# Differential attention on one core: stores from ScalarE's queue, loads in blocks, high parts first, and the norm factor by Newton's iteration on GpSimd

## The chip, the core and the metric

The kernel runs on one core of a Trainium2 chip. The metric is device time in microseconds (us) of one launch. The engines are named as in the profile: PE is TensorE's matmul, PEld its weight load, DVE is VectorE, ACT is ScalarE, POOL is GpSimd, SP is SyncE, which here only issues DMAs (SPq in a trace row; a DMA that ScalarE issues stands as ACTq).

## The reference

One layer of an encoder over two sequences (512 tokens and a second of the same length in the kernel's layout), width 1024, fp32: an S5 scan branch, a differential-attention branch and a cross-attention branch, gated and merged, then a gated FFN. The change lies in the differential attention and in the merge of its neighbours:

```python
def _diff_attention(q, k, v, lam, subln_g, lambda_init):
    ...
        s = jnp.einsum('bqhd,bkhd->bhqk', qblk, k).astype(jnp.float32) * scale
        probs = jax.nn.softmax(s, axis=-1).reshape(Bn, DIFF_HEADS, 2, Q_BLOCK, L)
        w = probs[:, :, 0] - lam * probs[:, :, 1]
        return jnp.einsum('bhqk,bkhe->bqhe', w.astype(v.dtype), v)
    ...
    o = _rmsnorm(o, subln_g) * (1.0 - lambda_init)
    return o.reshape(Bn, L, DIFF_WIDTH)

def _layer(x, mem, l, p):
    ...
    branches = (y_s5, y_diff, y_x)
    merged = None
    for n in range(N_BRANCH):
        term = jax.nn.sigmoid(g[..., n * D_MODEL:(n + 1) * D_MODEL]) * (branches[n] @ p['w_up'][l, n])
        merged = term if merged is None else merged + term
    x = x + merged @ p['w_out'][l]
```

## The kernel before

**Precision.** A product of fp32 values is made from three matmuls on parts: a value is cast on ScalarE to a high part (names ending in h or H) and VectorE subtracts that from it for the low part (l or L). The products are high by high, low by high and high by low; `mm3` issues them for the projections.

**Stages.** The S5 branch and the cross attention come first. The differential attention fills about 505 to 770 us of the span. It has 4 heads, 2 sequences and 4 query tiles of 128 rows, so 32 `steps`. Between its pieces, TensorE is kept at work by other units of the layer: projections of the next heads' q and k, of v, of the gates, and the merge of branches 0 and 2 (`units`, `qk_units`, `gate_units`, `merge_units`). They stand in `queue`, and `fill(n)` pulls from it.

**A step.** `score(i)` issues the scores of both maps of a step (PE into `bksc`, three banks in turn), VectorE's maximum `nb`, ScalarE's two exps `e`, and on VectorE the difference of the two maps and a transposition in blocks; the result is stored to `eD` in DRAM. For every second step `turn(i)` reads the pair of steps back from `eD` with four DMAs (`tn`), which completes the transposition. Such two steps are called a pair here: pair p holds steps 2p and 2p + 1. `settle` later issues the split of `tn` into pH (ScalarE's cast) and pL (VectorE's subtraction), and `outputs(i)`, three loop turns after the pair's second step, multiplies them by v in 12 matmuls into `bkoo`. After a head's four query tiles, `squares` makes the sums of squares `ss` (by TensorE's transposition and ScalarE's squares), and `normed` the factor: ScalarE's square root, VectorE's reciprocal, four transposes on TensorE that spread it over the partitions (`bktr`), VectorE's product, and a store to `bD`, from which the merge of branch 1 reads after the stage.

**Keys and queries.** A projection of q or k is rotated on VectorE and GpSimd; its split and its DMAs (tile `hl` to `q`, or to `h` and `l`, eight DMAs for each half of a key tile) are held back in a closure, `finished`, which `rotate` runs.

**Order.** A scheduler of the tile framework chooses the order of instructions on ScalarE, VectorE, GpSimd and SyncE from the program and its own costs. TensorE keeps the program's order here (`PE.on`). `tc.issue_after(x)` makes the instructions within it stand behind x where both are of the same engine. SyncE and ScalarE issue their instructions and DMAs strictly in the order so chosen, so one that waits holds all behind it.

Of the kernel before, what the change touches and what calls it, by code (L numbers as in the profile page):

```python
# [9 lines left out]

F32 = mybir.dt.float32
F32R = mybir.dt.float32r
I32 = mybir.dt.int32
AF = mybir.ActivationFunctionType
ALU = mybir.AluOpType
# [4 lines left out]
P = 128  # L20
L = 512
DM = 1024
KD = DM // P
# [47 lines left out]
def encoder(ctx: ExitStack, tc: tile.TileContext, a, out, out_t):  # L71
# [49 lines left out]
    wf = wp.tile([P, DM], F32, tag="wf", name="wf")  # L121
# [75 lines left out]

    last_mm = None

    def mm3(outs, wh, wl, xs, k, nk):  # L200

        nonlocal last_mm
        ws = slice(k * P, (k + 1) * P)
# [43 lines left out]
    def factor(ss, n, nt=4, bias=epsc):  # L247
        rs = root(ss, n, nt, bias)
        return rs, spread(rs, nt)
# [117 lines left out]
    o = bank()  # L367
# [344 lines left out]
        while any(g is g_ for g_ in queue):  # L712
            fill(1)

    def units(src, use, nk=KD, hl=lambda: (xh, xl)):

        wf = weight_in(src, nk * P)
        yield 0
        hi, lo = hl()
        wh, wl = weight_split(wf, nk * P)  # L720
        for s in range(NS):
            cs = slice(s * L, (s + 1) * L)
            o = bank()
            for k in range(nk):
                mm3([o], wh, wl, [(hi[k][:, cs], lo[k][:, cs])], k, nk)
# [128 lines left out]
    def rotate(*behind):  # L854
        with ExitStack() as es_:
            for b in behind:
                es_.enter_context(tc.issue_after(b.ins))
            while turning:
                turning.pop(0)()

    def rotated(is_q, first=False):


        names = (("q0", "q1"), ("h0", "h1", "l0", "l1"))[not is_q]
        tiles = [slot("qk", [P, NT], F32R, n_) for n_ in names]
        top, bottom = slice(0, 64), slice(64, P)

        def use(s, o):
            cs = slice(s * L, (s + 1) * L)
            t1 = rp.tile([P, L], F32, tag="nsq", name="t1", bufs=2) if first else ap_.tile([P, L], F32, tag="t1", name="t1", bufs=1)  # L870
            V.tensor_tensor(out=t1, in0=o, in1=rope[0], op=ALU.mult)
            t2 = ap_.tile([P, L], F32, tag="t2", name="t2", bufs=1)
            V.stream_shuffle(t2, o, mask)
            PO.tensor_tensor(out=t2, in0=t2, in1=rope[1], op=ALU.mult)
            PO.tensor_tensor(out=t1, in0=t1, in1=t2, op=ALU.add)
            def finished():
                hl = slot("ld", [P, 2, L], F32R, "hl")
                if is_q:
                    split(hl[:, 0], hl[:, 1], t1, scale=0.125)
                else:  # L880
                    split(*(by_row(hl[:, j], 4) for j in range(2)), by_tile(t1, 4))
                for mp in range(2):
                    for j in range(2):
                        src = hl[MAPS[mp], j].bitcast(F32)
                        if is_q:
                            SP.dma_start(tiles[mp].bitcast(F32)[MAPS[j], cs], src)
                        else:
                            for rows in (top, bottom):
                                SP.dma_start(tiles[2 * j + mp].bitcast(F32)[rows, cs], src)
# [30 lines left out]
        return list(zip(*(merge_part(n, t, tags[t]) for t in range(4))))  # L920

    def merge_units(n, b, m, first=False, last=False):
        u = units(a["w_up"][n, m], lambda s, o: use(s, o), 4, b)
        yield next(u)
        gt = slot("ld", name="gl")
        SP.dma_start(gt, gD[n * KD + m])
# [62 lines left out]
    def score(i):  # L989
        nonlocal last_e  # L990
        h, s, qt = steps[i]
        cs = slice(s * L, (s + 1) * L)
        if h and s == qt == 0:
            finish(dk[h])
            rotate()
        if qt == 0:
            s0[h, s] = acol.tile([P, 4], F32, tag="s0", name="s0", bufs=3)
        q_, k_, er = qk[h, True], qk[h, False], []
        qs_ = slice(s * L + qt * P, s * L + (qt + 1) * P)
        sc = [bank("sc") for _ in MAPS]  # L1000
        for mp in range(2):
            PE.matmul(sc[mp], q_[mp][:, qs_], k_[mp][:, cs], start=True, stop=False)
            PE.matmul(sc[mp], q_[mp][:, qs_], k_[2 + mp][:, cs], start=False, stop=True)
        for mp in range(2):
            er.append(softmax_parts(ap_, acol, sc[mp], L, 1.0, f"d{mp}", None if mp else s0[h, s][:, qt : qt + 1]))
        (e0, sm0), (e1, r1) = er
        V.scalar_tensor_tensor(out=r1, in0=r1, scalar=nlam, in1=sm0, op0=ALU.mult, op1=ALU.mult)
        V.scalar_tensor_tensor(out=e0, in0=e1, scalar=r1, in1=e0, op0=ALU.mult, op1=ALU.add)
        last_e = last_x, V.transpose(e1, e0)
        SP.dma_start(eD[i // 2 % 4, i % 2], e1)  # L1010

    def turn(i):
        h, s, qt = steps[i]
# [4 lines left out]
    def outputs(i):  # L1018

        h, s, qt = steps[i]  # L1020
        if h == 2 and s == qt - 1 == 0:
            finish(v1_)
        vh, vl = (v1 if h >= 2 else v0)[s]
        vs = slice((h % 2) * P, (h % 2) * P + P)
        pH, pL = pT.pop((h, s, qt // 2))
        if qt == 1:
            osb[h, s] = bank("oo")
        od = osb[h, s][:, qt // 2 * 2 * P : (qt // 2 + 1) * 2 * P]
        for j in range(4):
            PE.matmul(od, vh[:, j, vs], pH[:, j, :], start=(j == 0), stop=False)  # L1030
            PE.matmul(od, vh[:, j, vs], pL[:, j, :], start=False, stop=False)
            PE.matmul(od, vl[:, j, vs], pH[:, j, :], start=False, stop=(j == 3))
        if qt == 3:
            o_ = rp.tile([P, L], F32, tag="nsq", name="osb", bufs=2)
            S.copy(o_, osb[h, s])
            osb[h, s] = o_

    def squares(i):
# [9 lines left out]
        V.scalar_tensor_tensor(out=s0[h, s], in0=s0[h, s], scalar=EPS * P, in1=s0[h, s], op0=ALU.mult, op1=ALU.mult)  # L1048
        V.tensor_tensor(out=ss[h, s], in0=ss[h, s], in1=s0[h, s], op=ALU.add)

    def normed(i):
        h, s, _ = steps[i]
        _, bc = factor(ss[h, s], P, bias=0.0)
        V.scalar_tensor_tensor(out=osb[h, s], in0=osb[h, s], scalar=g04, in1=bc, op0=ALU.mult, op1=ALU.mult)
        SP.dma_start(bD[1, h, :, s * L : (s + 1) * L], osb[h, s])

    n = len(steps)
    for i in range(-1, n + 6):
        if i + 1 < n:
            score(i + 1)  # L1060
            settle(last_x)
            rotate(last_x)
        if i in (22, 23):
            first_in(2 * i - 44)
        fill(10)
        if i in (21, 22):
            first_in(3 if i == 21 else 1)
        if 0 <= i < n:
            turn(i)
        if 3 <= i < n + 3 and steps[i - 3][2] % 2:  # L1070
            outputs(i - 3)
# [1129 lines left out]
```

## Time and profile before

| | |
|---|---|
| median of 3 runs (lowest, highest) | 1571.77 us (1570.17, 1572.47) |
| the profiled execution: its time, its span | 1569.32 us, 1567.5 us |
| granted TensorE clock | 0.999 |
| busy share of the span: PE, PEld, DVE, ACT, POOL | 99%, 83%, 73%, 41%, 33% |
| the stage at 505 to 770 us: PE, DVE, ACT, POOL busy | 260.36, 207.61, 134.66, 47.58 us of 265.00 |
| exps of the stage on ACT | 64 of 686 ns |
| table loads of the stage on ACT | 13 of 1283 ns |

A row of the timeline gives the start (us of the span), the duration (us), the engine, the line, the operation, its output and inputs by the program's names, the tile, and in brackets how long the engine had been idle before and what ended that. In rows by group, the number behind the bar is the sum of busy time, then the mean in ns of one, then the idle time ahead of the group and what ended it. In a tile's rows, three numbers with slashes are the shortest, median and longest in ns. A row of waits gives the sum, the count and the mean in us. L62 is the line of the helper through which every engine's instructions are issued, so it doesn't tell operations apart; their tiles do.

### The profile page before, as it was taken

To read this page: it belongs to the slowest core of one execution; us is meant where nothing else is said; L and a number is where in the kernel's file an instruction comes from. 1 tells how busy PE (TensorE), PEld (TensorE's weight loads), DVE (VectorE), ACT (ScalarE), POOL (GpSimd) and SP (SyncE) were. 2 spreads that over 40 slices of the span, in tenths; PEclk is the share of its full clock that TensorE was granted. 3 is DMA by queue.
4 is the path that set the end of the run, shared out by engine and by line. 5 is a ranking of instruction groups with operands and counts; after the bars stand their busy time and mean duration, and the time that the engine had idled before them with its cause. 6 is when DMAs were issued, how large, how long until landed. Compare 5 with 4: busy or idle time off the path is not lost.

```text
span 1567.5 us, 21345 instructions
## 1 busy us (share of the span) xinstructions
PE 1553.6 (99%) x7505; PEld 1302.6 (83%) x7505; DVE 1141.2 (73%) x1769; ACT 637.0 (41%) x1109; POOL 513.5 (33%) x406
## 2 busy tenths in 40 slices
PE   9999999999999999999999999999999999999998
PEld 8888888888898888887888888888888888788887
DVE  6797689665774888877556567777777777999664
ACT  7354323344773356564223353333333323333222
POOL 0001000001443220200443345667665542445352
PEclk9999999999999999999999999999999999999999
DMA  9543372566897666577544324555433342786632
GB/s 364 205 148 136 105 254 103 177 179 217 278 306 221 176 204 185 172 239 266 189 148 170 139 94 143 185 177 175 155 122 134 115 154 77 261 292 203 208 118 107
DMA packets 162491, 286.22 MB, mean 183 GB/s; under 512 B 34768, under 2 KB 91344, under 8 KB 162384
## 3 DMA queue, kind: packets, MB, share of 16 engines
q1 hardware_dynamic: 160944, 280.64, 53.9%
q10 hardware_dynamic: 1440, 4.22, 0.7%
q8 instruction: 59, 0.97, 0.2%
q14 instruction: 48, 0.39, 0.1%
HBM read 185.47 MB, written 86.74 MB: 174 GB/s over the span
## 4 chain that ended last, share of the span: by engine, by line
PE 83%; DVE 6%; DMA 6%; issue 2%; ACT 2%; SPq 1%; DVEq 0%; ACTq 0%
PE bkmm L62 74%; PE bktr L62 7%; SPq L62 1%; DMA yt<-bD 1%; PE bksc L62 1%; PE bkoo L62 1%; DVE e L62 1%; DMA tn<-eD 1%; DVE wl L62 1%; DVE nb L62 1%; DMA c_n<-cD 1%; ACT e L62 1%; DMA eD<-e 1%; DMA zu<-uD 1%; DVE t L62 1%
## 5 line engine op out<-in xcount | busy, mean ns | idle before, releaser
L62 PE MATMUL bkmm<-xl,wh 128*128 128x512 f32 x640 | 250.7, 392 | 0.0
L62 PE MATMUL bkmm<-xh,wh 128*128 128x512 f32 x640 | 250.5, 392 | 0.0
L62 PE MATMUL bkmm<-xh,wl 128*128 128x512 f32 x640 | 249.6, 390 | 0.3 <-DVE wl L62 0.2
L62 PE MATMUL bkmm<-th,whl 128*128 128x512 f32 x696 | 227.3, 390 | 0.0
L62 ACT CAST wh<-wf 128x1024 fp32r<-128x1024 f32 (+1 forms) x131 | 116.0, 886 | 194.6 <-PE bkmm L62 164.2
L62 DVE TENSOR_TENSOR wl<-wf,wh 128x1024 fp32r<-128x1024 f32 (+1 forms) x132 | 141.5, 1073 | 54.7 <-ACT wh L62 52.1
L62 PEld LDWEIGHTS bkmm<-th,whl 128*128 128x128 f32 x696 | 130.6, 188 | 27.3 <-issue 0.2
L62 PEld LDWEIGHTS bkmm<-xh,wl 128*128 128x128 f32 x640 | 120.2, 188 | 26.2 <-DVE wl L62 1.1
L62 PE MATMUL bkmm<-th,w 128*128 128x512 f32 x432 | 139.6, 390 | 1.1 <-DVE nsq L62 1.1
L62 PEld LDWEIGHTS bkmm<-xh,wh 128*128 128x128 f32 x640 | 120.3, 188 | 24.1 <-issue 0.2
L62 PEld LDWEIGHTS bkmm<-xl,wh 128*128 128x128 f32 x640 | 120.3, 188 | 23.8 <-issue 0.6
L62 POOL TENSOR_TENSOR raw<-raw 128x128 f32<-128x128 f32 x144 | 92.2, 641 | 143.5 <-DMA raw<-in_w_fo 96.4
L62 PE MATMUL bkmm<-tl,whl 128*128 128x512 f32 x348 | 135.4, 389 | 0.0
L62 POOL TENSOR_TENSOR ws<-wf 128x512 f32<-128x512 f32 x44 | 72.6, 1650 | 146.0 <-DMA wf<-in_w_fu 139.1
L62 DVE TENSOR_TENSOR whl<-ws,whl 128x1024 fp32r<-128x1024 f32 x44 | 74.5, 1693 | 60.8 <-ACT whl L62 60.8
L62 PE MATMUL bkmm<-th,wh 128*128 128x512 f32 x260 | 101.3, 390 | 0.0
L62 PE MATMUL bkmm<-th,wl 128*128 128x512 f32 x260 | 101.2, 389 | 0.0
L62 PE MATMUL bkmm<-tl,wh 128*128 128x512 f32 x260 | 101.2, 389 | 0.0
L62 PEld LDWEIGHTS bkmm<-th,w 128*128 128x128 f32 x432 | 81.0, 188 | 19.1 <-DVE nsq L62 1.5
L62 POOL TENSOR_TENSOR mg<-mg,gl 128x1024 f32<-128x1024 f32 x16 | 44.2, 2762 | 131.8 <-DVE gl L62 127.1
L62 ACT ACTIVATE e<-bksc,nb 128x512 f32<-128x512 f32 (+1 forms) x96 | 58.7, 614 | 69.4 <-DVE nb L62 64.3
L62 PE MATMUL bkmm<-tl,w 128*128 128x512 f32 x216 | 84.0, 389 | 0.0
(644 smaller groups left out, 3580.2 us busy)
## 6 DMA issues: line engine op xcount, KB each, us to landing
wf<-in_w_in SPq DMA_DIRECT2D x40, 512.0 KB, 4.7
wD<-hl SPq DMA_DIRECT2D x36, 512.0 KB, 3.0
w<-wD SPq DMA_DIRECT2D x36, 512.0 KB, 3.9
gD<-gt SPq DMA_DIRECT2D x24, 512.0 KB, 3.1
gl<-gD SPq DMA_DIRECT2D x24, 512.0 KB, 3.8
raw<-in_w_fo SPq DMA_DIRECT2D x88, 128.0 KB, 3.5
wf<-in_w_fg SPq DMA_DIRECT2D x22, 512.0 KB, 3.9
wf<-in_w_fu SPq DMA_DIRECT2D x22, 512.0 KB, 3.5
```

The lines of the kernel that those rows point to most:

```text
L62: ins = do(*args, **kw)
```

## The change

It has five parts.

- Stores: the DMA that stores a step's result to `eD` is issued by ScalarE instead of SyncE for 31 of the 32 steps, and one step later, behind the second exp of the next step. `score` returns it as a closure.
- SyncE's order: the h and l DMAs stand behind the last load of `tn` that was issued before them, `rotate` runs after `turn`, and weight loads and gate loads get a position behind TensorE's last matmul of `mm3`. As that instruction is TensorE's and these DMAs are SyncE's, this last position changes no engine's order.
- High parts first: `outputs` issues the eight matmuls with pH, then the four with pL.
- Merge of branch 0: the row blocks are taken in the order 3, 0, 1, 2, which is the order in which they are loaded.
- Norm factor: `newton` on GpSimd makes one over the square root in 14 operations on 128x4 (a first value from the bits of the number, and three iterations), in place of ScalarE's square root and VectorE's reciprocal; `normed` runs one loop turn later. With the square roots, 13 table loads of ScalarE between 572 and 729 us go; one is added ahead of the next square root after the stage, that of `rs<-bktr` at 924 us.

The number of matmuls is the same. SyncE has 31 instructions fewer, ScalarE 11 more (31 DMAs in, square roots and table loads out), GpSimd 112 more, VectorE 8 fewer.

```diff
-        SP.dma_start(eD[i // 2 % 4, i % 2], e1)
+        return lambda: (S if i % 32 < n - 1 else SP).dma_start(eD[i // 2 % 4, i % 2], e1)
...
         for j in range(4):
             PE.matmul(od, vh[:, j, vs], pH[:, j, :], start=(j == 0), stop=False)
-            PE.matmul(od, vh[:, j, vs], pL[:, j, :], start=False, stop=False)
-            PE.matmul(od, vl[:, j, vs], pH[:, j, :], start=False, stop=(j == 3))
+            PE.matmul(od, vl[:, j, vs], pH[:, j, :], start=False, stop=False)
+        for j in range(4):
+            PE.matmul(od, vh[:, j, vs], pL[:, j, :], start=False, stop=(j == 3))
...
+    def newton(x):
+        y, t = (acol.tile([P, 4], F32, tag=t_, name=t_, bufs=2) for t_ in ("ny", "nt"))
+        PO.tensor_scalar(out=x, in0=x, scalar1=1.0 / P, scalar2=0.0, op0=ALU.mult, op1=ALU.add)
+        PO.tensor_scalar(out=y.bitcast(I32), in0=x.bitcast(I32), scalar1=-0.5, scalar2=1597463007.0, op0=ALU.mult, op1=ALU.add)
+        for _ in range(3):
+            PO.tensor_tensor(out=t, in0=y, in1=y, op=ALU.mult)
+            PO.tensor_tensor(out=t, in0=t, in1=x, op=ALU.mult)
+            PO.tensor_scalar(out=t, in0=t, scalar1=-0.5, scalar2=1.5, op0=ALU.mult, op1=ALU.add)
+            PO.tensor_tensor(out=y, in0=y, in1=t, op=ALU.mult)
+        return y
...
-        _, bc = factor(ss[h, s], P, bias=0.0)
+        bc = spread(newton(ss[h, s]))
...
-    for i in range(-1, n + 6):
+    stores = []
+    for i in range(-1, n + 7):
         if i + 1 < n:
-            score(i + 1)
+            store = score(i + 1)
             settle(last_x)
-            rotate(last_x)
+            if stores:
+                with tc.issue_after(last_x.ins):
+                    stores.pop()()
+            stores.append(store)
+        elif stores:
+            stores.pop()()
...
             turn(i)
+        rotate(last_x)
...
-        if i >= 6 and steps[i - 6][2] == 3:
-            normed(i - 6)
+        if i >= 7 and steps[i - 7][2] == 3:
+            normed(i - 7)
...
                             for rows in (top, bottom):
-                                SP.dma_start(tiles[2 * j + mp].bitcast(F32)[rows, cs], src)
+                                with tc.issue_after(last_t.ins):
+                                    SP.dma_start(tiles[2 * j + mp].bitcast(F32)[rows, cs], src)
...
-        u = units(a["w_up"][n, m], lambda s, o: use(s, o), 4, b)
+        u = units(a["w_up"][n, m], lambda s, o: use(s, o), 4, b, 3 if n == 0 else 0)
```

**The order on SyncE, at pair 1.** `tn<-eD` are the loads of a pair, `eD<-e` the store of a step, `h` and `l` the pieces of rotated keys. Before:

```order
L62 DMA tn<-eD 32x8x128
L62 DMA eD<-e 128x512
L62 DMA h_5470<-hl 64x512 x2
L62 DMA l_5472<-hl 64x512 x2
L62 DMA h_5471<-hl 64x512 x2
L62 DMA l_5473<-hl 64x512 x2
L62 DMA tn<-eD 32x8x128 x3
L62 DMA eD<-e 128x512
```

After:

```order
L62 DMA h_5469<-hl 64x512 x2
L62 DMA l_5471<-hl 64x512 x2
L62 DMA h_5470<-hl 64x512 x2
L62 DMA l_5472<-hl 64x512 x2
L62 DMA tn<-eD 32x8x128 x4
```

Pair 1's four loads, one of which stood ahead of the eight pieces of the keys' first half and three behind them, now stand together behind these pieces, and no store lies between.

**The order on ScalarE, at pair 1.** `e` are the exps (two for a step), `pH` the cast of pair 1, `hl` the split of rotated values, `gt` a gate, `wh` a weight's cast. Before:

```order
L62 ACTIVATE e,s_5559<-bksc,nb 128x512
L62 ACTIVATE e,sm<-bksc,nb 128x512
L62 ACTIVATE e,s_5559<-bksc,nb 128x512
L62 CAST hl<-t_5611 128x512
L62 ACTIVATE gt<-bkmm 128x512
L62 ACTIVATE e,sm<-bksc,nb 128x512
L62 CAST pH<-tn 128x1024
L62 CAST wh<-wf 128x1024
```

After:

```order
L62 ACTIVATE e,s_5569<-bksc,nb 128x512
L62 ACTIVATE e,sm<-bksc,nb 128x512
L62 CAST hl<-t_5610 128x512
L62 DMA eD<-e 128x512
L62 ACTIVATE gt<-bkmm 128x512
L62 CAST pH<-tn 128x1024
L62 ACTIVATE e,s_5569<-bksc,nb 128x512
L62 ACTIVATE e,sm<-bksc,nb 128x512
L62 DMA eD<-e 128x512
L62 CAST wh<-wf 128x1024
```

In both pieces the first two rows are the exps of step 5. Stores now stand behind the second exp of a step, and pair 1's pH, which stood behind both exps of step 6, stands ahead of them.

**The order on TensorE, in a pair's outputs.** The rows of pair 0:

```order
 L62 MATMUL bkoo<-pH,vh 128x256
-L62 MATMUL bkoo<-pL,vh 128x256
 L62 MATMUL bkoo<-pH,vl 128x256
 L62 MATMUL bkoo<-pH,vh 128x256
-L62 MATMUL bkoo<-pL,vh 128x256
 L62 MATMUL bkoo<-pH,vl 128x256
...
+L62 MATMUL bkoo<-pL,vh 128x256 x4
```

The first matmul that needs pL is the ninth of the twelve instead of the second.

More of the change, by code (lines that the diff above doesn't have):

```diff
@@ L11 @@
 F32 = mybir.dt.float32
-F32R = mybir.dt.float32r
+F32R, I32 = mybir.dt.float32r, mybir.dt.int32
 I32 = mybir.dt.int32
@@ L198, in encoder, with mm3 @@
     last_mm = None
-    def mm3(outs, wh, wl, xs, k, nk):
+    def mm3(outs, wh, wl, xs, k, nk, at=None):
         nonlocal last_mm
-        ws = slice(k * P, (k + 1) * P)
+        at = k if at is None else at
+        ws = slice(at * P, (at + 1) * P)
         for s, (xh, xl) in enumerate(xs):
@@ L713, in finish, with units @@
             fill(1)
-    def units(src, use, nk=KD, hl=lambda: (xh, xl)):
-        wf = weight_in(src, nk * P)
+    def units(src, use, nk=KD, hl=lambda: (xh, xl), first=0):
+        with tc.issue_after(last_mm.ins):
+            wf = weight_in(src, nk * P)
         yield 0
@@ L724, in units @@
             for k in range(nk):
-                mm3([o], wh, wl, [(hi[k][:, cs], lo[k][:, cs])], k, nk)
+                at = (k + first) % nk
+                mm3([o], wh, wl, [(hi[at][:, cs], lo[at][:, cs])], k, nk, at)
                 if k == nk - 1:
@@ L922, in merge_units @@
     def merge_units(n, b, m, first=False, last=False):
-        u = units(a["w_up"][n, m], lambda s, o: use(s, o), 4, b)
+        u = units(a["w_up"][n, m], lambda s, o: use(s, o), 4, b, 3 if n == 0 else 0)
         yield next(u)
         gt = slot("ld", name="gl")
-        SP.dma_start(gt, gD[n * KD + m])
+        with tc.issue_after(last_mm.ins):
+            SP.dma_start(gt, gD[n * KD + m])
         if first:
```

## The prediction

> **What bounds the kernel now.** The table of stretches was read first, over the stage that the change touches (differential attention, 505 to 770 us of the span); then the waits of TensorE in it, and last the timeline at each wait.
>
> ```profile
> 505.00:770.00 265.00, 260.36 (x1347) 220.25 (x1346) 207.61 (x352) 134.66 (x296) 47.58 (x30) 1.00 0.67 206
> ```
>
> The row gives length, then busy time of PE, PEld, DVE, ACT and POOL, the clock (1.00) and the DMA share. TensorE is idle for 265.00 − 260.36 = 4.64 us of the stage; ScalarE is busy for half of it, VectorE for 78%. The matmuls stay as many and as large. So the change can gain only what TensorE waits here, and can lose whatever new wait it makes. The waits:
>
> ```profile
> PE bkoo L62 <- DVE pL L62: 1.7, 2, 0.9
> PE bkoo L62 <- ACT pH L62: 0.9, 2, 0.5
> PE bkmm L62 <- DVE yl L62: 0.7, 1, 0.7
> PE bksc L62 <- ACT e L62: 0.6, 2, 0.3
> PE bkmm L62 <- DVE wl L62: 0.6, 1, 0.6
> ```
>
> Columns: sum, count, mean. They are eight events and 4.5 us, all of the idle time. But a matmul's modelled end hides part of a wait, so I measure from start to start. Two query tiles (steps) make a pair p, whose transposed weights come back from DRAM as `tn` and are split into pH and pL. Pair 1:
>
> ```profile
> 553.93 0.39 PE L62 MATMUL bkmm<-xl,wh 128*128 128x512 f32 x1
> 554.16 0.39 PE L62 MATMUL bkmm<-xh,wl 128*128 128x512 f32 x1
> 554.96 1.23 DVE L62 TENSOR_TENSOR pL<-tn,pH 128x1024 fp32r<-128x1024 f32 x1 [0.42 <-ACT pH L62]
> 554.98 0.39 PE L62 MATMUL bkoo<-pH,vh 128*128 128x256 f32 x1 [0.44 <-ACT pH L62]
> 556.24 0.39 PE L62 MATMUL bkoo<-pL,vh 128*128 128x256 f32 x1 [0.87 <-DVE pL L62]
> 556.47 0.28 PE L62 MATMUL bkoo<-pH,vl 128*128 128x256 f32 x1
> 556.59 0.28 PE L62 MATMUL bkoo<-pH,vh 128*128 128x256 f32 x1
> ```
>
> Unhindered, starts are 0.23 us apart at 512 columns (553.93 to 554.16) and 0.12 at 256 (556.47 to 556.59). So pair 1 loses 554.98 − 554.16 − 0.23 = 0.59 and 556.24 − 554.98 − 0.12 = 1.14: 1.73 us.
>
> ```profile
> 608.94 0.28 PE L62 MATMUL bkmm<-wh,xl 128*128 128x256 f32 x1
> 609.72 0.39 PE L62 MATMUL bkoo<-pH,vh 128*128 128x256 f32 x1 [0.49 <-ACT pH L62]
> 610.98 0.39 PE L62 MATMUL bkoo<-pL,vh 128*128 128x256 f32 x1 [0.87 <-DVE pL L62]
> 683.42 0.40 PE L62 MATMUL bkmm<-yh,wh 128*128 128x512 f32 x1
> 684.52 0.50 PE L62 MATMUL bkmm<-yl,wh 128*128 128x512 f32 x1 [0.70 <-DVE yl L62]
> ```
>
> Pair 5 in the same way: 0.66 + 1.14 = 1.80. The rest: yl 684.52 − 683.42 − 0.23 = 0.87, which is 0.17 above its wait in the row; with the same 0.17 for each, wl is 0.8 and the two for e are 0.6 + 0.34 = 0.9. Together 2.6. The ceiling of any gain is therefore 1.73 + 1.80 + 2.6 = 6.1 us, 0.39% of the span.
>
> **SyncE's order and the stores.** Why was pair 1 late? SyncE's queue (SPq):
>
> ```profile
> 543.44 0.37 SPq L62 DMA_DIRECT2D tn<-eD  x1
> 543.87 0.44 SPq L62 DMA_DIRECT2D eD<-e  x1
> 544.40 1.12 SPq L62 DMA_DIRECT2D h<-hl  x2
> ...
> 548.33 1.24 SPq L62 DMA_DIRECT2D l<-hl  x2
> 549.61 1.61 SPq L62 DMA_DIRECT2D tn<-eD  x3
> ```
>
> One load of pair 1 goes out at 543.44, then come the next step's store and eight pieces of rotated keys (h, l), and the other three loads only at 549.61 to 551.22; pL can begin behind pH at 554.96. Pair 5 has the same picture. After the change the four loads stand in one block, and the store isn't in this queue. The block may now stand behind the eight pieces (about 5.2 us: 544.40 to 549.57), but these can start earlier. By the order of the program, the eight pieces can go out once the store of step 3 has left this queue, some 5 us sooner; I put the block of pair 1 at 545 to 546.6 (a choice), landed by 550, pH near 551.5 and pL near 553, where the outputs want them at 554.4. Pair 5's h and l pieces move ahead in the same way. So both pairs' waits go: −3.5 us. Even with pH as late as now, the order of the outputs saves: eight matmuls with pH run before the first with pL, instead of one, so 7 × 0.12 = 0.84 us of each wait for pL is filled, 1.7 us for two.
>
> The price is paid on ScalarE. Its rows (sum and mean ns are behind the bar), SyncE's issues (ns least/median/most), and one store that ScalarE issues already:
>
> ```profile
> L62 ACT ACTIVATE e<-bksc,nb 128x512 f32<-128x512 f32 x64 | 43.6, 686 | 63.1 <-DVE nb L62 58.0 <-issue 3.6 <-ACT e L62 1.4
> L62 ACT CAST pH<-tn 128x1024 fp32r<-128x1024 f32 x16 | 16.7, 1046 | 16.4 <-DMA tn<-eD 16.4
> L62 ACT ACT_TABLE_LOAD x13 | 16.7, 1283 | 0.2
> L62 SPq DMA_DIRECT2D eD<-e x32: 319/338/542, 516.6 to 725.2; - x32
> L2096 ACTq DMA_DIRECT2D yD<-y__2108 x1: 336/336/336, 296.0 to 296.0; - x1
> ```
>
> 31 stores × 0.336 = 10.4 us go onto ScalarE, of which they take time only where it isn't idle; SyncE is rid of 31 × 0.338 = 10.5 us. A store's own data (the transpose of e) can be late and would hold ScalarE; that is why it stands one step later, behind the second exp of the next step, when the transpose is done. So I cost the wait at nothing, except that each store leaves some 2 to 4 us later than it did. A pair's second store follows its step by about 6.5 us (32 steps over 516.6 to 725.2: 208.6 / 32), so the loads do too; 14 of the 16 pairs had room and show no wait.
>
> **The differential factor.** Away from ScalarE go the square roots of eight norms, and their table loads: 13 less one that now stands ahead of a later square root, at 924: 12 × 1.283 = 15.4 us. That is more than the stores add, so ScalarE is 5 us lighter, at no matmul's gain as such: ScalarE waits 63.1 us for VectorE's nb ahead of the exps already. The load put ahead of the later square root costs 1.28 us at most, once; I take zero, since its factor isn't among TensorE's waits. A page of the Trainium skill (ScalarE: Activation LUTs, What ACT_TABLE_LOAD costs) adds a drain to the load, 2.66 us for each switch; the rows show 0.2 us idle ahead of all 13 loads. By the page ScalarE would be freed of 32 us, and TensorE of no more than the two waits for e.
>
> GpSimd gets 8 × 14 operations on 128x4. No row shows one of that size there; the nearest are these, and where the result is wanted:
>
> ```profile
> L62 POOL TENSOR_TENSOR raw<-raw 128x128 f32<-128x128 f32 x144 | 92.2, 641 | 143.5 <-DMA raw<-in_w_fo 96.4 <-issue 19.8 <-DVE nb L62 14.3
> L62 POOL COPY fs<-tl 128x1 f32<-128x1 f32 x1 | 1.1, 1119 | 10.0 <-DVE tl L62 10.0
> L2193 POOL MEMSET const-float32-0.0<- 128x1 f32 x1 | 0.1, 98 | 0.2 <-issue 0.2
> 570.01 0.14 DVE L62 TENSOR_TENSOR ss<-ss,s 128x4 f32<-128x4 f32 x1
> 578.68 0.60 PE L62 MATMUL bktr<-ident,rs 128*128 128x128 f32 x4
> 749.26 2.77 POOL L62 TENSOR_TENSOR mg<-mg,gl 128x1024 f32<-128x1024 f32 x1 [88.49 <-DVE gl L62]
> 750.11 1.95 DVE L62 TENSOR_TENSOR ss<-ss,s 128x4 f32<-128x4 f32 x1 [0.33 <-ACT acc L62]
> 756.91 0.60 PE L62 MATMUL bktr<-ident,rs 128*128 128x128 f32 x4
> ```
>
> The chain of one norm lies between two ends: 14 × 0.098 = 1.4 us and 14 × 1.119 = 15.7 us. The 1.119 was a lone copy; the 128x4 work differs from raw (641 ns for 128 columns) by its columns, so I lie nearer the low end, at 0.36 each: 5 us. The factor is wanted today 8.5 us behind ss (570.15 to 578.68), for the last norm 4.9 us (752.06 to 756.91). The transposes now come one loop turn later, some 26 matmuls × 0.23 = 6 us: room of 14.5 us, and about 11 for the last. 5 us fits; cost zero. The cover is gone above 0.79 to 1.04 us an operation.
>
> **The other edits.** The gates' and weights' new position marks refer to a matmul, thus to another engine than the one that issues these DMAs, and move nothing. Merging branch 0 with row block 3 first meets a part that was loaded first; it may take the yl wait (0.87) away. The norm one turn later makes its last store later by about 5 us; its reader, the merge of branch 1, comes after branches 0 and 2, and I take zero, at most the 1 to 2 us that a late `w_up` cast would cost.
>
> **The sum.** −3.5 (pairs 1 and 5) −1.5 (of 2.6: yl, and half of the rest, since ScalarE is lighter) +0.7 (one or two new waits like the present ones for e, 0.3 to 0.5 each, where a store or a cast now stands ahead of an exp) = −4.3 us. The profiled execution took 1569.3 us, so 1565.0. The median of the runs shown is 1571.8, 2.4 above it; hence 1567.5 (−0.27%). A measurement tells about 0.2% (3.1 us) from no change, so this is just past it.
>
> **Rivals.**
>
> First: the waits are replaced, not removed. SyncE's blocks put all four loads behind the h and l pieces, pair 1 or another pair is late in its place, and only the 1.7 us from the order of the outputs stays, less some new 0.3. For it: the pieces take 5.2 us, and a pair has no room beyond its own. Against: 14 pairs had none today. 1571.8 − 1.4 = 1570.4.
>
> Second, on the other side: ScalarE becomes a bound by its order. The store goes out a step later, so `tn` lands later, but pH keeps its place among ScalarE's instructions. Where `tn` isn't there, ScalarE stands at pH, and the exps behind it come late; then TensorE's next scores wait for a bank. ScalarE stands 16.4 us for `tn` already over 16 casts (row above), about 1 us each, and e comes late twice by 0.3. How far an exp comes ahead:
>
> ```profile
> 536.91 0.69 ACT L62 ACTIVATE e<-bksc,nb 128x512 f32<-128x512 f32 x1 [2.81 <-DVE nb L62]
> 539.78 0.39 PE L62 MATMUL bksc<-h,q 128*128 128x512 f32 x1
> ```
>
> The scores at 539.78 reuse the bank that this exp left at 537.60: a lead of 2.2 us. It decides when a pair's loads land more than that later in relation to pH's place than today. If eight of the 16 pairs then cost 1 us, +8 − 4.3 = +3.7: 1575.5. Also for it: pair 1's pH now stands ahead of step 6's exps, not behind them. Against: fewer DMAs stand ahead of the loads on SyncE, and most pairs' pH keep their place.
>
> Third: GpSimd's chain is late. VectorE and GpSimd hinder each other: the last ss took 1.95 us instead of 0.14 while GpSimd ran mg (rows above). If each of the 14 operations were held to the length of the copy, 15.7 us stand against room of 14.5 (seven norms) and 11 (the last): 7 × 1.2 + 4.7 = 13.1, less 4.3: 1580.6. The Trainium skill (SBUF — State Buffer, Who interferes with whom) states that the two engines take turns at a shared port for whole instructions, which the ss row bears out; no run here shows such small operations on GpSimd.
>
> Fourth: no change within the measurement for want of critical waits: the pairs' waits go and as many arise at exps, 1571.
>
> **How the numbers follow.** The forecast −4.3 has 0.46. First and fourth rival: 0.31. Second: 0.18. Third: 0.05. The forecast reaches from all 6.1 us gained (1565.7) down to 1564.5 by the scatter of the runs (1.2), and up to −2 (1569.8); the second rival ends at 1575.5. The range 1564.5 to 1575.5 leaves out the third and the larger forms of the second, under 0.2. Faster by over 0.2%: the forecast's larger part 0.40 and a little of the first rival's, 0.44. Within: 0.34. Slower: the second and the third, 0.22.
>
> **What would show it.** Right: in the waits of TensorE over the stage no bkoo row for pL or pH, pair 1's `tn` loads in one row x4, no table load between 572 and 729 us, 14 short GpSimd operations behind each ss that end before bktr, idle time of the stage near 1 to 1.5 us. Wrong: new rows bksc for e (second rival), longer idle of ScalarE at pH for `tn` than 16.4 us, bktr for ny (third), or bkoo rows at other pairs (first).

## The result: slower by 0.75%, and the profile after

| | before | after |
|---|---|---|
| median (lowest to highest) | 1570.96 us (1570.17 to 1572.47), 6 runs | 1582.90 us (1581.24 to 1586.54), 6 runs |
| ratio, 95% interval | | 1.0075 [1.0062, 1.0087] |
| the profiled execution: time, span | 1569.32, 1567.5 us | 1582.01, 1580.2 us |

The forecast of 1567.5 us and its range up to 1575.5 were wrong, and on the wrong side. The page of the changed kernel, span and busy times:

```profile
span 1580.2 us, 21429 instructions
PE 1555.9 (98%) x7505; PEld 1303.6 (82%) x7505; DVE 1139.3 (72%) x1761; ACT 620.4 (39%) x1089; POOL 545.5 (35%) x518
```

TensorE has as many matmuls as before. ScalarE's busy time fell by 637.0 − 620.4 = 16.6 us (table loads and square roots; the DMA issues that it took on are not counted as busy), so a less busy ScalarE came with a longer span. The waits of TensorE in the stretch from 500 to 790 us follow. The third figure of such a row is the longest wait, not the mean as was said ahead of the result; the sums and counts, on which the forecast rests, are not touched by that.

```profile
PE bksc L62 <- ACT e L62: 10.8, 9, 2.5
PE bktr L62 <- DVE osb L62: 4.2, 1, 4.2
```

No row names pL, pH, yl or wl any more. Nine waits for an exp (two of 0.6 us together before) and one for VectorE's `osb` took their place. Measured from start to start, as in the prediction (every step between two matmuls that is 0.15 us or more above the usual step of its shape; steps too long by 0.15 to 0.23 us put down to the slower rate below), the stretch lost 6.4 us before and 17.0 + 1.6 = 18.6 us after. The difference, 12.2, is nearly all of the 12.7 us by which the span grew.

**Where the exps became late.** Groups of ScalarE and VectorE from 505 to 790 us (behind the last bar the idle time ahead of the group); the first two rows are after, the third is before (pH before stands in the prediction):

```profile
L62 ACT CAST pH<-tn 128x1024 fp32r<-128x1024 f32 x16 | 16.8, 1048 | 26.5 <-DMA tn<-eD 26.2 <-issue 0.3
L62 DVE TENSOR_TENSOR pL<-tn,pH 128x1024 fp32r<-128x1024 f32 x16 | 20.0, 1250 | 20.3 <-ACT pH L62 16.2 <-DMA h<-hl 4.0
```
```profile
L62 DVE TENSOR_TENSOR pL<-tn,pH 128x1024 fp32r<-128x1024 f32 x16 | 19.5, 1222 | 9.1 <-ACT pH L62 8.9
```

ScalarE now stands 26.2 us in front of pH for `tn` (16.4 before), and VectorE 20.3 us in front of pL (9.1 before). One pair shows the chain, pair 9, in the timeline of the changed kernel:

```profile
644.66 0.70 DVE L62 STREAM_TRANSPOSE e<-e 128x512 f32<-128x512 f32 x1
...
647.91 0.68 ACT L62 ACTIVATE e<-bksc,nb 128x512 f32<-128x512 f32 x1
647.93 0.33 ACTq L62 DMA_DIRECT2D eD<-e  x1
...
652.25 1.81 SPq L62 DMA_DIRECT2D tn<-eD  x4
...
657.02 1.05 ACT L62 CAST pH<-tn 128x1024 fp32r<-128x1024 f32 x1 [3.31 <-DMA tn<-eD]
...
658.11 1.68 DVE L62 TENSOR_TENSOR pL<-tn,pH 128x1024 fp32r<-128x1024 f32 x1 [2.78 <-ACT pH L62]
...
662.13 1.24 DVE L62 TENSOR_REDUCE nb<-bksc 128x1 f32<-128x512 f32 x2
662.81 0.69 ACT L62 ACTIVATE e<-bksc,nb 128x512 f32<-128x512 f32 x1 [3.27 <-DVE nb L62]
...
663.64 0.50 PE L62 MATMUL bksc<-h,q 128*128 128x512 f32 x1 [2.49 <-ACT e L62]
```

The transposed weights are ready at 645.36; the store goes out at 647.93, behind the next step's exps; the loads go out at 652.25, and ScalarE stands 3.31 us until they land. VectorE's pL starts late, and so do the maximum nb, which stands behind pL in VectorE's queue, and the exp; TensorE waits 2.49 us for the bank that the exp frees. The same pair in the kernel before:

```profile
644.02 0.70 DVE L62 STREAM_TRANSPOSE e<-e 128x512 f32<-128x512 f32 x1
644.75 0.33 SPq L62 DMA_DIRECT2D eD<-e  x1
...
646.78 1.84 SPq L62 DMA_DIRECT2D tn<-eD  x4
```

There the store left 0.03 us after the transpose, against 2.57 us now, and the loads 5.5 us earlier than after the change. Over the 32 stores the median went from 0.03 to 2.05 us behind the transpose. In pair 9 the exps weren't pushed by ScalarE alone: it was the two together, pH and pL, each at the head of an engine's queue.

Not all of the 10.8 us came this way. Followed back through the timeline in the same manner, four of the nine waits (to 608.16, 663.64, 692.73 and 707.16, 6.6 us together) begin at a pH that stands for `tn`. The wait of 1.98 us to 679.64 begins at ScalarE's cast of `yt`, which stood 2.56 us for its own load, and that of 1.35 us to 721.63 at VectorE's product `mg`, which stood 2.00 us for a gate's load. The three smallest, 0.9 us together, have other beginnings.

**Where the single long wait comes from.** The `bktr` tiles of the norm and of the squares share one PSUM bank (`open_banks(mm=3, sc=3, tr=1, oo=1)`). After the change:

```profile
727.76 0.60 PE L62 MATMUL bktr<-ident,ny 128*128 128x128 f32 x4
...
732.08 1.23 DVE L62 TENSOR_TENSOR pL<-tn,pH 128x1024 fp32r<-128x1024 f32 x1 [2.85 <-ACT pH L62]
...
735.77 0.74 DVE L62 SCALAR_TENSOR_TENSOR osb<-osb,g,bktr 128x512 f32<-128x512 f32 x1
...
736.65 0.74 PE L62 MATMUL bktr<-ident,osb 128*128 128x128 f32 x4 [4.18 <-DVE osb L62]
```

The norm's factor fills the bank at 727.76, and VectorE reads it only at 735.77, having stood 2.85 us in front of pL for pair 14's pH, which itself stood 3.08 us for `tn`. The next head's squares, which want the bank, wait 4.18 us. In the kernel before, the norm came two loop turns ahead of these squares; now one.

**Half rate behind it.** The stretch that ends with that wait and the one behind it, as in the table of stretches:

```profile
733.62:737.03 3.41, 0.38 (x4) 0.41 (x5) 3.31 (x6) 1.57 (x2) 0.00 (x0) 1.00 0.88 318
737.03:740.45 3.42, 3.42 (x11) 2.74 (x10) 2.48 (x5) 1.15 (x8) 0.60 (x4) 0.50 0.50 180
```

The granted clock (third number from the end) is 0.50 for 3.42 us behind the wait, and 1.00 again from 740.45. In the slow stretch matmuls of 512 columns start 0.43 us apart instead of 0.23, which adds 1.6 us. The Trainium skill (TensorE: Matmul & The Clock Gate, Part 1) says that the array falls to half its clock after an idle window of about 3.4 us and needs about as long a busy one to come back. The trace agrees in rate and duration; that it needs a full 3.4 us of idleness is not borne out: in the run with the stores alone (below) the clock was 0.50 behind a wait of 2.1 us.

### The profile page after: what moved, and what is told of

It is laid out like the page before. It is cut to its first block, busy times and chain, and to the rows that moved or that the text cites. A ratio compares the mean times of both kernels' runs of the same rounds, so it can differ in the third digit from the quotient of the medians.

```text
span 1580.2 us, 21429 instructions
## 1 busy us (share of the span) xinstructions
PE 1555.9 (98%) x7505; PEld 1303.6 (82%) x7505; DVE 1139.3 (72%) x1761; ACT 620.4 (39%) x1089; POOL 545.5 (35%) x518
## 4 chain that ended last, share of the span: by engine, by line
PE 80%; DMA 7%; DVE 6%; SPq 2%; issue 2%; ACT 1%; POOL 1%; DVEq 0%; ACTq 0%; POOLq 0%
PE bkmm L62 72%; PE bktr L62 7%; SPq L62 2%; DMA tn<-eD 1%; DMA eD<-e 1%; DMA gl<-gD 1%; DVE e L62 1%; DVE nb L62 1%; PE bkoo L62 1%; PE bksc L62 1%; ACT e L62 1%; DMA c_n<-cD 1%; DVE t L62 1%; DMA zu<-uD 1%; DVE wl L62 1%
## 5 line engine op out<-in xcount | busy, mean ns | idle before, releaser
L62 PEld LDWEIGHTS bkmm<-xl,wh 128*128 128x128 f32 x640 | 120.3, 188 | 23.8 <-issue 0.6
L62 ACT CAST whl<-ws 128x1024 fp32r<-128x1024 f32 x44 | 46.0, 1045 | 83.4 <-PE bkmm L62 73.9
```

What stands on the lines that cost most here:

```text
L62: ins = do(*args, **kw)
```

## The experiments

Each ratio is against the kernel before, which ran on the same chip beside it; medians in us. The ratio is that of the record and need not be the quotient of two medians. Waits and "slower rate" are measured from start to start as above, from 500 to 790 us.

| kernel | median | ratio, 95% interval | waits + slower rate |
|---|---|---|---|
| before | 1569.7 to 1571.0 | | 6.2 + 0.2 |
| after | 1582.90 | 1.0075 [1.0062, 1.0087] | 17.0 + 1.6 |
| after, stores from SyncE at once | 1572.45 | 1.0017 [1.0005, 1.0030] | 8.6 + 0.4 |
| after, ScalarE's square root | 1585.36 | 1.0097 [1.0082, 1.0112] | 18.6 + 1.9 |
| after, split one step later | 1571.89 | 1.0008 [0.9999, 1.0018] | 6.5 + 1.4 |
| before, stores late from ScalarE | 1575.73 | 1.0040 [1.0025, 1.0055] | 8.5 + 1.7 |
| after, norm at its old place | 1574.37 | 1.0029 [1.0016, 1.0042] | 10.3 + 1.8 |
| after, split later and norm at its old place | 1577.35 | 1.0049 [1.0035, 1.0064] | 10.4 + 2.6 |
| before, Newton at the norm's old place | 1568.53 | 0.9990 [0.9981, 1.0000] | 5.8 + 0.2 |
| before, Newton, outputs' and merge order | 1568.98 | 0.9996 [0.9986, 1.0007] | 5.6 + 0.4 |
| before, norm one turn later | 1572.56 | 1.0024 [1.0013, 1.0035] | 7.5 + 1.8 |
| before, Newton, outputs' and merge order, norm one turn later | 1575.32 | 1.0041 [1.0026, 1.0056] | 10.2 + 2.4 |
| after, stores from SyncE, not held | 1574.62 | 1.0031 [1.0020, 1.0042] | 9.5 + 1.8 |
| after, stores from SyncE at once, split later | 1574.27 | 1.0022 [1.0010, 1.0034] | 7.9 + 2.8 |

The span of each goes with its last column: it lies within 3 us of 1567.5 plus what that column has more than 6.4. The column misses half rate where matmuls have 256 columns, as their steps grow from 0.12 to 0.21 us, less than the 0.15 that it counts from: another 1.5 us each in "before, stores late from ScalarE", in "before, Newton at the norm's old place" and in "after, split later and norm at its old place", and 2.1 in "after, ScalarE's square root".

The scheduler makes a new order for each kernel, so a run differs from its neighbour by more than the edit. How much that weighs is seen where two cures together come out 2 to 5 us slower than either (below).

### The stores back on SyncE, in their own step

```diff
-        return lambda: (S if i % 32 < n - 1 else SP).dma_start(eD[i // 2 % 4, i % 2], e1)
+        SP.dma_start(eD[i // 2 % 4, i % 2], e1)
+        return lambda: None
```

> The changed kernel with the stores of eD back on SyncE and issued in their own step; the loads in blocks, the order of the outputs, the merge order and Newton's iteration stay. Theory A (the store that leaves a step later brings tn late, ScalarE stands at pH and VectorE at pL, and the exps behind them come late): 1568 to 1572 us, ScalarE's idle time at pH for tn back from 26.2 to about 16 us, rows bksc for e in TensorE's waits under 3 us instead of 10.8. Rival B (Newton's iteration and what it shifts on GpSimd and VectorE): 1580 to 1583. Rival C (SyncE's blocks and the later rotate): 1578 to 1582.

10.5 us of the loss of 12 go (1572.45, just past the upper end expected). TensorE's waits and ScalarE's row:

```profile
PE bksc L62 <- ACT e L62: 5.7, 6, 2.1
PE bktr L62 <- DVE osb L62: 1.8, 1, 1.8
L62 ACT CAST pH<-tn 128x1024 fp32r<-128x1024 f32 x16 | 16.8, 1048 | 19.2 <-DMA tn<-eD 19.1
```

The late stores carry most of it, as theory A had it, but not all: the rows for e fell to 5.7, not under 3. Two events make up most of those. One at 581.8: ScalarE's split `hl` stands ahead of the exps and waits for GpSimd's rotation.

```profile
580.44 0.63 ACT L62 ACTIVATE hl<-t 128x512 fp32r<-128x512 f32 x1 [4.84 <-POOL t L62]
580.97 0.67 ACT L62 ACTIVATE e<-bksc,nb 128x512 f32<-128x512 f32 x1
```

In the kernel before, the exp of this step stood ahead of that split. The rotation is late itself: VectorE had its input ready at 574.93, but GpSimd was in Newton's chain until 577.77. So this wait needs the new order and Newton's chain, which is a piece of rival B. The other is at 677, behind a pH that stood 4.2 us for `tn`. It speaks for a piece of rival C, that the order of keys and loads adds waits too; no run has SyncE's order alone, so that stays argued.

### ScalarE's square root instead of Newton's iteration

```diff
-        bc = spread(newton(ss[h, s]))
+        _, bc = factor(ss[h, s], P, bias=0.0)
```

> The changed kernel with ScalarE's square root and VectorE's reciprocal in place of Newton's iteration, still one loop turn later. Theory A (late stores): 1580 to 1585 us, nothing gained; the 13 table loads come back on ScalarE and may cost 0 to 2 us more. Rival B (Newton's iteration): 1570 to 1573. Rival C (SyncE's blocks): 1580 to 1585.

1585.36, slower still by 2.5, just past the range of theory A, with 12.0 us of waits for e. Newton's iteration isn't the cause. That it helps beside the late stores is likely only, as the two intervals overlap (1.0062 to 1.0087 with it, 1.0082 to 1.0112 without).

### The split one step later

```diff
-            settle(last_x)
+            if i % 2 or i == 30:
+                settle(last_x)
```

> The changed kernel with the split of tn into pH and pL issued one step later, the stores as late as in the change. Theory A: the loads are then there when ScalarE comes to pH; ScalarE's idle time at pH for tn falls from 26.2 to under 8 us, the rows bksc for e fall to under 3 us, and the time to 1566 to 1572 us, if the outputs don't come to wait for pH or pL in their turn (then bkoo rows, some 1 us each). Rivals B and C: the waits at e stay, 1579 to 1583.

1571.89: 11 us of the 12 go, though the stores leave as late as in the change and still cost ScalarE their 31 issues. The waits and ScalarE's row:

```profile
PE bktr L62 <- DVE osb L62: 2.5, 1, 2.5
PE bkoo L62 <- ACT pH L62: 1.5, 2, 1.0
PE bksc L62 <- ACT e L62: 0.7, 2, 0.4
PE bkoo L62 <- DVE pL L62: 0.5, 2, 0.2
L62 ACT CAST pH<-tn 128x1024 fp32r<-128x1024 f32 x16 | 16.7, 1043 | 2.1 <-DMA tn<-eD 2.1
```

So neither a late store nor its issue on ScalarE has to cost: here pH of 14 of the 16 pairs stands behind one more step's exps than in the change, ScalarE stands 2.1 us there, and the exps are in time. The edit shifted other operations too (of VectorE's 313 instructions of the stage beside those of pL and the norms, 29 don't keep the common order), so the 11 us are those of the whole new order. What is left is osb's 2.5 us, the slower rate behind it, and outputs that wait for pH in two pairs.

### The stores alone, in the kernel before

```diff
-        SP.dma_start(eD[i // 2 % 4, i % 2], e1)
+        return lambda: (S if i % 32 < n - 1 else SP).dma_start(eD[i // 2 % 4, i % 2], e1)
...
+            if stores:
+                with tc.issue_after(last_x.ins):
+                    stores.pop()()
+            stores.append(store)
```

> The kernel before with one edit: the stores of eD on ScalarE's queue, one step later. Theory A: it carries the loss by itself, 1578 to 1584 us, with rows bksc for e of 6 us and more. Rivals B and C: 1570 to 1573.

1575.73, about half of the loss that was expected, and 3.5 us of waits for e instead of 6 or more:

```profile
PE bksc L62 <- ACT e L62: 3.5, 3, 2.0
PE bkmm L62 <- DVE mg L62: 2.5, 2, 2.0
```

The stores cost 5.2 us here and 10.5 in the change: they need the other edits for the rest. ScalarE stands 20.1 us at pH for `tn` (16.4 before), but the two longest waits begin elsewhere: 1.96 us for e at ScalarE's cast of `yt`, which stands 3.06 us for its load, and 2.04 us for mg at a gate's load.

Where the edits meet is seen at pair 5. In the kernel before, and here, its pH stands behind both exps of step 14. In the five kernels that have the change's order on SyncE and the split in its old step, pH of pairs 1 and 5 stands ahead of exps which it stood behind before. Pair 5's pH then stood 4.87 us for `tn` with the late stores, and TensorE waited 2.53 us for the exp behind it; with the stores at once it stood 1.51 us, and the wait was 0.45. With the stores alone no exp waits there.

The clock behind the wait of 2.1 us for e (to 682.27), in the stretch behind it:

```profile
683.73:687.14 3.41, 3.41 (x9) 2.67 (x9) 2.95 (x5) 3.28 (x6) 0.00 (x0) 0.50 0.49 182
```

### The norm's place

```diff
-    for i in range(-1, n + 7):
+    for i in range(-1, n + 6):
...
-        if i >= 7 and steps[i - 7][2] == 3:
-            normed(i - 7)
+        if i >= 6 and steps[i - 6][2] == 3:
+            normed(i - 6)
```

The changed kernel with the norm where it was before:

> The changed kernel with the norm one loop turn earlier again, where it stood before (Newton's iteration and all else stay). Theory A2 (the norm one turn later holds the one bktr bank until VectorE's osb, which stands behind a late pL, so that the next squares wait 4.2 us, and TensorE runs eight matmuls at about half its rate behind that wait): the row bktr for osb goes, 1576 to 1579 us; the waits for e stay near 11 us. Rival: the place of the norm is of no weight, the wait turns up elsewhere (bktr for ny, Newton's chain being too long for the shorter room), 1581 to 1585.

1574.37: 8.5 us less by this edit, more than the 4 to 7 expected. Its waits:

```profile
PE bksc L62 <- ACT e L62: 4.1, 4, 2.0
PE bktr L62 <- POOL ny L62: 2.6, 2, 1.5
PE bkmm L62 <- DVE mg L62: 1.4, 1, 1.4
PE bktr L62 <- ACT osb L62: 0.9, 1, 0.9
```

The wait for VectorE's osb is gone, as A2 has it. The rows for e fell by 6.7 too, and those for ny come up. That fall is not in A2. It is larger than what the bank gave back (4.2 us), and 4.9 us of other rows came. The order is a new one, and other pairs are late by other amounts; the two effects were not separated, so the 8.5 us are not the price of the bank.

The same with the late split:

> The changed kernel with the split of tn one step later and the norm where it stood before. Theories A and A2 together: no bktr row, no large rows for e, 1566 to 1569 us, below the kernel before. Rival: the outputs wait for pH instead, or Newton's chain ends too late (bktr for ny), 1570 to 1574.

1577.35, a miss by 8 us: the two cures together are worse than either. A row `bkmm <- DVE mg` of 3.5 us, pH and pL in two pairs (2.6) and 2.6 us of slower rate came up. Why VectorE's mg came late there was not followed further.

The norm one turn later, alone in the kernel before (the reverse diff):

> The kernel before with one edit: the norm one loop turn later (ScalarE's square root stays). Theory A2 says that this holds the one bktr bank across the next squares, and that it costs where VectorE's osb is late; in the kernel before pL is seldom late, so 1570 to 1573 us, at most one small row bktr for osb. Rival (the place of the norm costs by itself, whatever the stores do): 1575 to 1579, as much as its removal from the change gained (8.5).

1572.56, by 0.24% slower and within the range. But osb waits only 0.2 us; what is new is one wait for e of 2.7 us, with the slower rate after it (1.8). It doesn't come from the bank: ScalarE's later square root brings a table load and a gate ahead of that exp.

```profile
685.58 1.28 ACT L62 ACT_TABLE_LOAD   x1
...
686.88 0.60 ACT L62 ACTIVATE gt<-bkmm 128x512 f32<-128x512 f32 x1
687.37 0.68 ACT L62 ACTIVATE e<-bksc,nb 128x512 f32<-128x512 f32 x1
...
688.20 0.50 PE L62 MATMUL bksc<-h,q 128*128 128x512 f32 x1 [2.68 <-ACT e L62]
```

### Newton's iteration alone, and three edits together

Newton in the kernel before, with the norm at its old place:

```diff
-        _, bc = factor(ss[h, s], P, bias=0.0)
+        bc = spread(newton(ss[h, s]))
```

> The kernel before with one edit: Newton's iteration on GpSimd for the norms' factor, at the norm's old place. Theory (Newton's iteration helps since 12 table loads leave ScalarE): 1567 to 1570 us. Rival (it is neutral here, and what it won beside the late stores was only room on a crowded ScalarE): 1570 to 1572. Rival (its chain of 14 is late for the room of 4.9 us at the last norm): 1572 to 1575.

1568.53, 0.10% less with an interval that touches no change: a small gain at most. Its chain is late twice (`bktr <- POOL ny`, 2.0 us), where it wins the yl, wl and e rows.

With the outputs' high parts first and branch 0 from row block 3 added:

> The kernel before with three edits and its own stores, loads and rotate: the outputs' high parts first, Newton's iteration at the old place, and branch 0 merged from row block 3. If the waits of the kernel before are its only loss (6.1 us) and these edits make none: 1566 to 1569 us, with the waits for pL about 0.84 us shorter each. Rival: the scheduler's order shifts and new waits take their place, 1570 to 1573.

1568.98, not told apart from before. The order of the outputs does what the prediction said: pL is 0.27 and 0.20 us late from start to start in pairs 1 and 5, instead of 1.14 twice. But pH of pair 5 is later (1.5 us instead of 0.65), and ny 1.95 and 1.65. The last norm on GpSimd:

```profile
753.24 2.37 POOL L62 TENSOR_TENSOR mg<-mg,gl 128x1024 f32<-128x1024 f32 x1
755.57 0.20 POOL L62 TENSOR_TENSOR ny<-ny,nt 128x4 f32<-128x4 f32 x1
755.82 0.65 PE L62 MATMUL bktr<-ident,ny 128*128 128x128 f32 x4 [1.49 <-POOL ny L62]
```

The chain's last operation stands behind a merge addition of 2.37 us in GpSimd's queue. So the last norm is late by one long operation between the 14, not by their own length. The other late one (to 685.01) has nothing between: four of its operations took 0.51 to 1.18 us instead of 0.2, and the chain 6.3 us (678.67 to 684.96) instead of the 3.8 of the quickest.

The same with the norm one turn later:

> The kernel before with the outputs' high parts first, branch 0 from row block 3, and Newton's iteration with the norm one turn later. Against the same with the norm at its old place the two rows bktr for ny (3.3 us) must go if they come from the chain's length: 1565 to 1568 us. Rival: a row bktr for osb takes their place, as in the change, 1569 to 1572.

1575.32, past both ranges: 6.3 us slower than with the norm at its old place, in a kernel whose stores are not late. The rows for ny go, as expected, but osb takes their place at a higher price (4.9 us against 3.3, and 2.0 us more of the slower rate):

```profile
PE bktr L62 <- DVE osb L62: 4.9, 2, 3.8
PE bksc L62 <- ACT e L62: 1.7, 3, 0.9
PE bkoo L62 <- ACT pH L62: 1.5, 2, 1.2
```

So with Newton's iteration the norm's later place costs 6.3 us, and the wait for the single bank is the largest of its rows. With ScalarE's factor the later place cost 2.5 us, and there the one long wait came by the table load above and not by the bank. This run has one figure more: ScalarE stands 23.8 us at pH for `tn`, with stores in their old place, and e waits only 1.7 us. The sum of idle time in front of pH is not a price; it counts where exps stand behind it without a lead.

### Two more places for the stores

The stores written one step later, but issued by SyncE:

```diff
-        return lambda: (S if i % 32 < n - 1 else SP).dma_start(eD[i // 2 % 4, i % 2], e1)
+        return lambda: SP.dma_start(eD[i // 2 % 4, i % 2], e1)
```

> The changed kernel with the stores written one step later as in the change, but issued by SyncE, where the mark behind ScalarE's exp doesn't hold them, so that each leaves when its transpose is done and SyncE comes to it. Theory A (what costs is that the store goes out behind ScalarE's next exps): 1571 to 1576 us, ScalarE's idle time at pH for tn near 19 us. Rival (the written place, one step later, costs through the scheduler's order, not ScalarE's queue): 1579 to 1584.

1574.62, near the run with stores at once and within theory A's range, with 15.3 us of ScalarE at pH for `tn`. The stores leave 0.03 us (median) behind their transposes, as in the kernel before: it is the place behind ScalarE's next exps that makes a store late, not where it is written.

The stores at once from SyncE and the split later:

> The changed kernel with the stores at once from SyncE and the split of tn one step later. Theory A: with loads early and the split late, ScalarE waits under 2 us at pH for tn, no large rows for e; 1566 to 1570 us, if only bktr for osb stays. Rival: the late split makes the outputs wait for pH as it did in pairs 1 and 9 of the run with the late split alone, 1570 to 1574.

1574.27, a miss: ScalarE stands only 3.5 us for `tn` and e costs 1.8, but osb costs 4.8 in two places and the slower rate 2.8. So the stores at once give nothing more once the split is late, and the bank is the largest wait that remains.

## Why the prediction was wrong, step by step

- **Pairs 1 and 5 (−3.5): right at the outputs, but half of it was paid elsewhere.** No bkoo row is left; pair 1's loads went out from 546.12, pH began at 550.48 and pL at 551.85, each about 1 us from the forecast. The estimate for the order of the outputs alone (0.84 for each wait for pL) measured 0.87 and 0.94. But pair 5's pH came from behind two exps to ahead of them (603.78 instead of 608.62), and the 1.80 us won were lost again, and more, in the 2.53 us at the exp. So waits were replaced and not removed, as the first rival had it, though by another way than it gave. The blocks on SyncE were not needed either: with the stores alone 0.4 us of bkoo waits are left.
- **"I cost the wait at nothing": the step that failed.** The prediction took the 14 pairs without a wait at the outputs as room for late loads. But the room that counted was not TensorE's. pH and pL stand at fixed places in ScalarE's and VectorE's queues, ahead of exps and maxima, and the 16.4 us at pH were quoted as a row and read as harmless idle time. With the stores some 2 us later (2.5 in pair 9), they rose to 26.2 us and VectorE's 9.1 to 20.3. Taking the late stores out gives back 10.5 of the 12 us; moving pH and pL behind the next exps, with the stores as late as before, 11. The delay itself was forecast rightly (2 to 4 us); that it is free was not.
- **The second rival had the mechanism, but not its size.** It was given 0.18, with ScalarE's stand at pH pushing exps past their lead; it was priced at +3.7 net where +12 was measured. It counted eight events of 1 us. There were nine of 10.8 us by the rows (12.3 from start to start), four of which, 6.6 us, go back to pH; two of these are 2.5 us, because VectorE's nb stood behind pL as well. And it left out the bank and the half rate.
- **"The norm one turn later ... I take zero": failed.** It looked at the store to `bD` and not at the PSUM bank that the factor holds. That was 4.3 us from start to start, and 1.6 of half rate. The run that puts the norm back gains 8.5 us, but 6.7 us of waits for e go with it, so the bank's own share is not separated.
- **The two failures overlap.** Removing either the late stores (10.5), the late pH (11.0) or the norm's place (8.5) takes away most of the loss; the sum is more than 12. In the change osb is late because VectorE stands at pL. The stores alone make 5.2. What joins them to 12 is in part the place of pH: pair 5's wait of 2.5 us needs both the late store and pH ahead of the exps. How much more of it is the order that the scheduler makes afresh for each kernel stays open; the two runs with two cures each, 1577.35 and 1574.27, show that such orders alone can be worth several us.
- **Newton's iteration: the price was right, the gain is small.** The groups of its six kinds in the changed kernel add up to 31.2 us for 112 operations, 0.28 each (0.36 was the estimate); from the first to the last of the 14, a chain took 4.3 to 8.6 us (5 was the estimate). Beside the late stores the median is 2.5 us lower with it, hardly clear of the scatter; alone it saves between nothing and 0.19%. A cost that the prediction didn't have: its chain stands in GpSimd's queue ahead of a rotation of keys, where one exp came late by it (2.1 us, with the stores back on SyncE). Third rival: single operations were held to 1.28 us, but 96 of the 112 were not, and the chain was late by up to 2 us, not by 13. The 2.66 us that the Trainium skill (ScalarE: Activation LUTs, What ACT_TABLE_LOAD costs) gives a switch are not borne out. In the kernel before, 0.2 us of idle time stand ahead of all 13 loads, and behind seven of them the next operation begins within 0.02 us, so no drain is seen on either side; ScalarE's busy time fell by 16.6 us with 12 loads and eight square roots fewer.
- **−1.5 for yl and the rest:** yl and wl are gone, but in the run with Newton alone also, without the merge order. So that credit to row block 3 was not shown.
- **A loose reading.** Of the 63.1 us that ScalarE stands ahead of the exps, 58.0 end with nb; 63.1 is all idle time there. The sum doesn't use it.

## What to carry to other kernels

Before a producer is delayed, read where its consumer stands in an in-order queue: an engine's idle time in front of an operation that waits for a DMA is not free room if exps or maxima that have no lead are queued behind it. Move the consumer with the producer. When a step is moved one turn, list what it holds (here the only PSUM bank of its kind) and how many turns are left until the next owner. And where a scheduler orders the program afresh, compare the orders before a difference of a few us is put down to one edit.

## What was not expected of the hardware

- A wait of TensorE can cost more than itself, and where it falls decides. In the fourteen traces the half rate came in pieces of 3.41 us (three times of 6.83), 1.3 to 1.7 us dearer than at full clock for each 3.41, and within a trace these pieces lie on one grid: with the stores alone they begin at 594.98 and 683.73, 26 times 3.413 us apart. Laid on that grid, each of the 15 falls of the clock from 500 to 790 us followed a piece in which TensorE had lost at least 1.86 us from start to start, in one wait or in several. No piece at full clock in which it lost over 2.02 us went without a fall; between the two both happened. So the wait of 2.5 us to 608.16 in the changed kernel left the clock alone: the grid cuts it at 607.33, with 1.87 us on one side and 0.83 on the other. The 4.2 us before 736.65 had 3.0 in one piece. This is read off these traces; no run varied it.

```profile
603.90:607.33 3.43, 1.72 (x13) 1.29 (x11) 2.46 (x4) 1.42 (x3) 0.00 (x0) 1.00 0.68 161
607.33:610.74 3.41, 2.58 (x19) 2.50 (x20) 2.42 (x6) 1.92 (x5) 0.00 (x0) 1.00 0.20 77
```

- Operations of 128x4 on GpSimd mostly took 0.19 to 0.20 us, but up to 1.28 us; in the changed kernel all 16 of the 112 that took over 0.4 us ran beside an operation of VectorE (1.18 us at 658.66, beside a pL). That VectorE is what lengthened them was not tried. The row of one kind, least/median/most in ns:

```profile
L62 POOL TENSOR_TENSOR ny<-ny,nt x24: 200/202/1279, 570.7 to 771.2; 128x4 f32<-128x4 f32 x24
```
